# A bidirectional two-branch encoder layer: block products by Strassen's scheme in stages through DRAM

## Chip, cores and metric

One core of one Trainium2 chip. The metric is the device time of one execution of the kernel in microseconds, as the median over runs; lower is better. Engines are named as in the profile: PE is TensorE's matmul, PEld its weight load, DVE is VectorE, ACT is ScalarE, POOL is GpSimd, SP is SyncE, which issues DMAs.

## What is computed

A layer on `x` of 1024 rows (time) by 1024 columns, all in float32:

```
p = x @ w_in                         # 10272 columns in 13 parts
GLA   : 4 heads,  keys 128, values 256; decays log_sigmoid(low-rank @ up + bias) / 16
HGRN2 : 8 heads,  keys 128, values 128; f = lb + (1 - lb) * sigmoid(.), key = 1 - f, decay f
both  : forward and backward chunked linear attention, summed;
        per-head RMSNorm * silu(gate); product with a 1024 x 1024 branch matrix
y   = (sigmoid(m_gla) * y_gla + sigmoid(m_hgrn) * y_hgrn) @ w_out
out = LayerNorm(2 ** 0.25 * x + y)
```

The decays are multiplied up within segments of 64 time steps: with b the running product, `scores = (q * b) (k / b)^T`, masked; a state per chunk carries the rest.

## The kernel before

Class `Layer` does the whole layer in one pass in SBUF. Rows and columns are handled in blocks of 128 (`P`); `T` and `D` are 1024, `KC` and `NT` are 8. `load_x` (L164) keeps x transposed, k on the partitions, as eight pairs of tiles `xh`, `xl`: a float32r part and the rest, made by `split` (L88), a cast on ScalarE (L91) and a subtraction (L92, on GpSimd or VectorE). Each weight block is split in the same way, and a float32 product is formed as three float32r products, hi x hi, hi x lo, lo x hi.

`product_t` (L205) makes a narrow product, 128 output columns by 1024 times: 8 k x 3 terms x 2 halves = 48 matmuls of 512 columns (L216). `narrow` (L221) is called for q and k of the GLA heads, q and the two forget gates of the HGRN heads, and the 16 blocks of merge gates. `wide` (L225) makes 256 output columns with time on the partitions, for values and gates: 2 x 4 x 24 matmuls of 256 columns (L243), sixteen times.

`heads` (L679) goes through four GLA heads, then eight HGRN heads; each head computes its own projections right where it needs them. `scaled` (L339) forms, per direction, the running product of the decays in segments of 64 (a scan, L348, with `FLOOR` to restart each segment), its reciprocal on VectorE in four pieces of 256 columns (L363), the rescaling to the chunk's middle (L364, L365), and the multiplications with q (L366, GpSimd) and k (L368, L370). `attend` (L453) makes masked scores (`scores`, L373), the backward states, then the forward states and the outputs chunk by chunk (`states`, L599; products at L566), the norm and the gate, and transposes the result, which goes to DRAM as `oa` or `oh`. In the GLA heads the values, keys, scores and states are split in halves too (`split_values`, `transposed_halves`, `pieces`) and each of their products is three float32r products; in the HGRN heads they are plain float32.

`branches` (L735) computes merge gates and the two branch products (L216 again), `final` (L777) the output product (L814), residual and LayerNorm. After the heads, `judge` (L838) checks the smallest decay product and the largest mean square; if one is out of bounds, the layer is done again by a slower exact path under `tc.If` (L885).

The order on each engine is set by a scheduler of the framework (L942), from the program's order, from priorities (`high_priority` at L90, L260 and others) and from a simulated timeline. Input loads go over SP's queue; `oa` and `oh` are stored from ScalarE's queue (L531).

Of the kernel before, what the change touches and what calls it, by code (L numbers as in the profile page):

```python
# [9 lines left out]
F32 = mybir.dt.float32  # L10
F32R = mybir.dt.float32r
I32 = mybir.dt.int32
AF = mybir.ActivationFunctionType
ALU = mybir.AluOpType
AX = mybir.AxisListType

P = 128
T = 1024
D = 1024
KC = D // P  # L20
# [26 lines left out]
class Layer:  # L47
    def __init__(self, tc, io, exact):
        self.tc, self.nc, self.io, self.exact = tc, tc.nc, io, exact
# [26 lines left out]
    def t(self, tag, shape=(P, T), dt=F32, name=None):  # L76
        bufs = self.BUFS.get(tag, 1)
        if self.exact and tag in ("PF", "PB"):
            bufs = 1
        return self.sb.tile(list(shape), dt, tag=tag, name=name or tag, bufs=bufs)  # L80
# [4 lines left out]
    def att_ps(self):  # L85
        return self.ps.tile([P, 512], F32, tag="att", name="att", bufs=4)
# [7 lines left out]
    def consts(self):  # L94
        nc = self.nc
        self.ident = self.t("ident", (P, P))
        make_identity(nc, self.ident)
        self.zero = self.t("Z")
        nc.vector.memset(self.zero, FLOOR)
        self.prm = self.t("prm", (P, 43))  # L100
        self.mhalf = self.t("mhalf", (P, NT))
        nc.vector.memset(self.mhalf, -0.5)
        self.minp = self.t("minp", (P, 24))
        self.msall = self.t("msall", (P, 96))
        if self.exact:
            self.level_masks()
        else:
            self.masks()
# [55 lines left out]
    def load_x(self):  # L164
        nc = self.nc
        self.xh, self.xl = [], []
        low = self.io["wn"][0]
        raw = self.raw((P, KC, P))
        hi, lo = self.pair()
        self.ready = [(hi, None)]  # L170
        parts = [slice(0, 2), slice(2, KC)]

        def weights(s):
            nc.sync.dma_start(out=raw[:, s, :], in_=low[:, s, :])
            with self.tc.high_priority():
                nc.scalar.copy(hi[:, s, :], raw[:, s, :])
                nc.gpsimd.tensor_tensor(
                    out=hi[:, s, 96:], in0=raw[:, s, 96:], in1=hi[:, s, 96:].bitcast(F32), op=ALU.subtract
                )

        weights(parts[0])
        for k in range(KC):
            if k % 2 == 0 and k < 4:
                pair = self.t(("gate", "v")[k // 2], (P, 2, T))
            xr = pair[:, k % 2, :] if k < 4 else self.t(("A", "KT", "N0", "N1")[k - 4])
            h = self.t(f"xh{k}", dt=F32R)
            l = self.t(f"xl{k}", dt=F32R)
            for s in (slice(0, 512), slice(512, T)) if k == 0 else (slice(0, T),):
                nc.sync.dma_start(out=xr[:, s], in_=self.io["xT"][k][:, s])
                self.split(h[:, s], l[:, s], xr[:, s], nc.vector)  # L190
            self.xh.append(h)
            self.xl.append(l)
            if k == 1:
                weights(parts[1])
                nc.sync.dma_start(out=self.prm, in_=self.io["prm"])
                self.ready.append(self.weights(self.io["wn"][NARROW.index(A_Q)]))
# [67 lines left out]
    def values(self, column):  # L264
        v = self.t("v", (P, NT, 256))
        for g, ps in self.wide(column):
            with self.tc.high_priority():
                self.nc.scalar.copy(v[:, 4 * g : 4 * g + 4, :], ps)
        return v

    def gates(self, column):
        nc = self.nc
        gate = self.t("gate", (P, NT, 256))
        for g, ps in self.wide(column):
            out = gate[:, 4 * g : 4 * g + 4, :]
            with self.tc.high_priority():
                nc.scalar.activation(out, ps, AF.Sigmoid)
                nc.vector.tensor_tensor(out=out, in0=ps, in1=out, op=ALU.mult)
        return gate
# [59 lines left out]
    def scaled(self, q, k, f, omlb, d, index):  # L339
        nc = self.nc  # L340
        pr = self.t("PB" if d else "PF")
        first, last = (63, 0) if d else (0, 63)
        seg = lambda a: a.rearrange("p (s j) -> p s j", j=64)
        z = self.zero
        nc.vector.tensor_scalar_max(seg(z)[:, :, first], seg(f)[:, :, first], FLOOR)
        nc.vector.memset(seg(f)[:, :, first], 0.0)  # L346
        step = -1 if d else 1
        nc.vector.tensor_tensor_scan(  # L348
            out=pr[:, ::step], data0=f[:, ::step], data1=z[:, ::step], initial=0.0, op0=ALU.mult, op1=ALU.max
        )  # L350
        nc.vector.memset(seg(z)[:, :, first], FLOOR)
        ends = self.t(f"ends{d}", (P, NT, 2))
        nc.vector.tensor_copy(out=ends.rearrange("p c h -> p (c h)"), in_=seg(pr)[:, :, last])
        nc.vector.tensor_reduce(
            out=self.minp[:, index : index + 1], in_=ends.rearrange("p c h -> p (c h)"), axis=AX.X, op=ALU.min
        )
        mid = self.t(f"mid{d}", (P, NT))
        nc.vector.reciprocal(mid, ends[:, :, d])
        half = lambda a: a.rearrange("p (c h j) -> p c h j", h=2, j=64)[:, :, d, :]
        bc = lambda a: a.unsqueeze(2).to_broadcast([P, NT, 64])  # L360
        for n in range(4):
            r = slice(256 * n, 256 * n + 256)
            nc.vector.reciprocal(f[:, r], pr[:, r])  # L363
        nc.vector.tensor_tensor(out=half(f), in0=half(f), in1=bc(ends[:, :, d]), op=ALU.mult)  # L364
        nc.vector.tensor_tensor(out=half(pr), in0=half(pr), in1=bc(mid), op=ALU.mult)  # L365
        nc.gpsimd.tensor_tensor(out=pr, in0=pr, in1=q, op=ALU.mult)  # L366
        if omlb is None:
            nc.vector.tensor_tensor(out=f, in0=f, in1=k, op=ALU.mult)  # L368
        else:
            nc.vector.scalar_tensor_tensor(out=f, in0=f, scalar=omlb, in1=k, op0=ALU.mult, op1=ALU.mult)  # L370
        return pr, f, ends
# [70 lines left out]
    def prepare(self, head, q, kf_of):  # L442
        a = self.t("A") if self.exact else None
        parts = []
        for d in range(2):
            f, k, omlb = kf_of(d)
            if self.exact:
                parts.append(self.exact_dir(a, q, k, f, d, d == 0))
            else:
                parts.append(self.scaled(q, k, f, omlb, d, 2 * head + d))  # L450
        return a, parts
# [112 lines left out]
    def product(self, out, terms):  # L564
        for i, (l, r) in enumerate(terms):
            self.nc.tensor.matmul(out, l, r, start=(i == 0), stop=(i == len(terms) - 1))  # L566
# [80 lines left out]
    def gla_front(self, h):  # L647
        nc = self.nc
        ps = self.narrow(A_Q + P * h)
        q = self.t("Q")  # L650
        with self.tc.high_priority():
            nc.scalar.mul(q, ps, QSCALE)
        fs = self.decays.pop(h) if h in self.decays else self.gla_decays(h)
        ps = self.narrow(A_K + P * h)
        k = self.t("K")
        with self.tc.high_priority():
            nc.scalar.copy(k, ps)
        v = self.values(A_V + 256 * h) if self.exact else self.split_values(A_V + 256 * h)
        prepared = self.prepare(h, q, lambda d: (fs[d], k, None))
        gains = [self.prm[:, 40:41], self.prm[:, 41:42]]  # L660
        rows = [self.oa[2 * h], self.oa[2 * h + 1]]
        return lambda gate: self.attend(h, prepared, v, 0, 256, gate, gains, rows)
# [64 lines left out]
    def merge_gate(self, column, i, sig):  # L727
        ps = self.narrow(column + P * i)
        with self.tc.high_priority():
            self.nc.scalar.activation(sig, ps, AF.Sigmoid)  # L730
# [141 lines left out]
        self.final()  # L872


@with_exitstack
def kernel(ctx: ExitStack, tc: tile.TileContext, xT, x, wn, ww, up_f, up_b, prm, wbg, wbh, w_out, ln_g, ln_b, out):
    io = dict(
        xT=xT, x=x, wn=wn, ww=ww, up_f=up_f, up_b=up_b, prm=prm, wbg=wbg, wbh=wbh, w_out=w_out, ln_g=ln_g, ln_b=ln_b, out=out
    )
    with ExitStack() as inner:  # L880
        fast = Layer(tc, io, False)
        fast.open(inner)
        fast.run()
        bad = fast.unsafe()
    with tc.If(bad > 0):  # L885
        with ExitStack() as inner:
            exact = Layer(tc, io, True)
            exact.open(inner)
            exact.run()
# [56 lines left out]
```

## Time and profile before

| | |
|---|---|
| median of 3 runs | 1405.22 us (1404.96 to 1405.34) |
| the profiled execution's own time | span 1404.6 us from the first to the last instruction |
| busy: PE / PEld | 1369.2 / 1217.4 us |
| busy: DVE / ACT / POOL | 722.5 / 508.6 / 405.9 us |
| instructions | 20453 |
| HBM read / written | 73.16 / 12.58 MB |

How to read it: an engine's busy time is the union of its instructions' spans. Matmuls are pipelined, so that the mean duration of one is longer than the distance from one to the next. A float32 matmul appears as two records, a float32r one as one. A group names the tile written, then the tiles read, with partitions x elements and type; behind the bar it has busy time and mean duration, then the idle time before it. The window table has a column per engine, the granted clock of TensorE as a share of full speed, the DMA engines' busy share and the bytes moved.

### The profile page before, as it was taken

The page shows a single profiled execution, that of the slowest core. Times are in us where ns is not written, and L with a number is a line of the kernel's source. Part 1 is how long each engine was busy: PE and PEld are TensorE (multiplying, and loading weights), DVE is VectorE, ACT ScalarE, POOL GpSimd, SP SyncE. Part 2 cuts the span into 40 slices and gives each one's busy share as a digit, 9 for nine tenths or more (in the row PEclk, how much of TensorE's full clock was granted, in tenths as well). Part 3 has the DMA queues.
Part 4 walks back from the last instruction along what each step waited for, and adds up shares of the span by engine and source line. Part 5 has one row for each costly group of instructions (what it writes and reads, how often), then busy time and mean ns, then how long its engine had stood idle before and what let it go on. Part 6 is the DMA issues. An engine that isn't in the chain of part 4 may idle for free.

```text
span 1404.6 us, 20453 instructions
## 1 busy us (share of the span) xinstructions
PE 1369.2 (97%) x8721; PEld 1217.4 (87%) x8721; DVE 722.5 (51%) x993; ACT 508.6 (36%) x822; POOL 405.9 (29%) x262
## 2 busy tenths in 40 slices
PE   8999999999999999999999999999999999999996
PEld 6989979989999889888988898988888888888886
DVE  5886478296255575557545654565311132123744
ACT  6445365454453434334333443243421031113100
POOL 3334425326233231323132313222222222221111
PEclk9999999999999999999999999999999999999998
DMA  6010110210112110211021102011231151113421
GB/s 224 25 46 31 61 46 16 76 46 31 61 47 75 46 46 16 76 46 45 16 76 31 60 16 76 31 46 60 91 105 45 46 177 48 45 46 105 136 105 63
DMA packets 24405, 87.16 MB, mean 62 GB/s; under 512 B 2928, under 2 KB 3056, under 8 KB 24304
## 3 DMA queue, kind: packets, MB, share of 16 engines
q1 hardware_dynamic: 22000, 77.36, 16.6%
q10 hardware_dynamic: 2304, 8.39, 1.6%
q8 instruction: 70, 1.15, 0.3%
q14 instruction: 31, 0.25, 0.1%
HBM read 73.16 MB, written 12.58 MB: 61 GB/s over the span
## 4 chain that ended last, share of the span: by engine, by line
PE 66%; DVE 16%; POOL 5%; issue 5%; ACT 5%; DMA 3%; SPq 0%; POOLq 0%; DVEq 0%; ACTq 0%
PE proj L216 35%; PE proj L243 13%; PE att L566 7%; PE proj L814 5%; DVE FF L363 4%; DMA wraw<-in_dram 3%; DVE FB L363 2%; POOL PB L366 2%; PE att L382 2%; POOL wlo L92 2%; DVE PF L348 2%; ACT whi L91 1%; POOL PF L366 1%; PE att L540 1%; DVE PB L348 1%
## 5 line engine op out<-in xcount | busy, mean ns | idle before, releaser
L92 POOL TENSOR_TENSOR wlo<-wraw,whi 128x1024 fp32r<-128x1024 f32 x78 | 187.4, 2402 | 447.7 <-ACT whi L91 447.7
L243 PE MATMUL proj<-whi,xh 128*128 128x256 f32 x1024 | 291.2, 284 | 1.5 <-DVE v L261 1.5
L243 PE MATMUL proj<-wlo,xh 128*128 128x256 f32 x1024 | 291.1, 284 | 0.2 <-POOL wlo L92 0.2
L243 PE MATMUL proj<-whi,xl 128*128 128x256 f32 x1024 | 291.2, 284 | 0.0
L216 PE MATMUL proj<-xh,whi 128*128 128x512 f32 x768 | 243.7, 395 | 0.7 <-DVE FB L346 0.5
L216 PE MATMUL proj<-xl,whi 128*128 128x512 f32 x768 | 241.5, 394 | 0.0
L216 PE MATMUL proj<-xh,wlo 128*128 128x512 f32 x768 | 239.4, 391 | 0.0
L91 ACT CAST whi<-wraw 128x1024 fp32r<-128x1024 f32 x78 | 81.9, 1050 | 357.9 <-PE proj L216 176.9
L243 PEld LDWEIGHTS proj<-whi,xh 128*128 128x128 f32 x1024 | 196.1, 191 | 2.6 <-DVE v L261 2.0
L243 PEld LDWEIGHTS proj<-wlo,xh 128*128 128x128 f32 x1024 | 196.1, 191 | 1.2 <-POOL wlo L92 0.5
L243 PEld LDWEIGHTS proj<-whi,xl 128*128 128x128 f32 x1024 | 196.1, 191 | 0.0
L216 PEld LDWEIGHTS proj<-xh,wlo 128*128 128x128 f32 x768 | 144.2, 188 | 30.3 <-POOL wlo L92 0.3
L216 PEld LDWEIGHTS proj<-xh,whi 128*128 128x128 f32 x768 | 143.3, 189 | 30.3 <-ACT whi L91 0.9
L216 PEld LDWEIGHTS proj<-xl,whi 128*128 128x128 f32 x768 | 143.5, 189 | 29.4 <-issue 0.7
L92 POOL TENSOR_TENSOR wlo<-N,whi 128x1024 fp32r<-128x1024 f32 x18 | 43.7, 2429 | 149.7 <-ACT whi L91 149.7
L363 DVE RECIPROCAL FF<-PF 128x256 f32<-128x256 f32 x48 | 79.7, 1707 | 0.1
L363 DVE RECIPROCAL FB<-PB 128x256 f32<-128x256 f32 x48 | 79.7, 1708 | 0.1
L366 POOL TENSOR_TENSOR PB<-PB,Q 128x1024 f32<-128x1024 f32 x12 | 41.5, 3457 | 83.6 <-DVE PB L365 81.0
L91 ACT CAST whi<-N 128x1024 fp32r<-128x1024 f32 x19 | 19.9, 1050 | 106.2 <-PE proj L216 56.4
L566 PE MATMUL att<-v,KT 128*128 128x128 f32 (+1 forms) x392 | 56.1, 282 | 0.8 <-DVE KT L557 0.7
L631 ACT ACTIVATE V<-att,ends 128x128 f32<-128x128 f32 (+1 forms) x144 | 54.5, 392 | 6.0 <-PE att L566 5.9
L566 PEld LDWEIGHTS att<-v,KT 128*128 128x128 f32 x392 | 51.8, 194 | 3.3 <-DVE KT L557 1.7
(364 smaller groups left out, 2173.5 us busy)
## 6 DMA issues: line engine op xcount, KB each, us to landing
wraw<-in_dram SPq DMA_DIRECT2D x82, 512.0 KB, 3.5
N<-in_dram SPq DMA_DIRECT2D x24, 512.0 KB, 3.5
oa<-KT ACTq DMA_DIRECT2D x8, 512.0 KB, 3.3
oh<-KT ACTq DMA_DIRECT2D x8, 512.0 KB, 3.4
whi<-in_dram SPq DMA_DIRECT2D x8, 512.0 KB, 3.5
out_dram<-wlo SPq DMA_DIRECT2D x7, 512.0 KB, 2.6
v<-oh SPq DMA_DIRECT2D x4, 512.0 KB, 5.4
v<-in_dram SPq DMA_DIRECT2D x2, 512.0 KB, 7.6
```

The source lines that it names most:

```text
L91: nc.scalar.copy(hi, raw)
L92: (lo_engine or nc.gpsimd).tensor_tensor(out=lo, in0=raw, in1=hi.bitcast(F32), op=ALU.subtract)
L216: nc.tensor.matmul(out, w[:, k, :], x[k][:, 512 * n : 512 * n + 512], start=(i == 0), stop=(i == len(terms) - 1))
L243: nc.tensor.matmul(ps[:, 256 * j : 256 * j + 256], x[k][:, P * c : P * c + P], w[k], start=(k == 0 and i == 0), stop=(k == KC - 1 and i == 2),
L348: nc.vector.tensor_tensor_scan(out=pr[:, ::step], data0=f[:, ::step], data1=z[:, ::step], initial=0.0, op0=ALU.mult, op1=ALU.max)
L363: nc.vector.reciprocal(f[:, r], pr[:, r])
L366: nc.gpsimd.tensor_tensor(out=pr, in0=pr, in1=q, op=ALU.mult)
L382: mm = lambda out, l, r: nc.tensor.matmul(out, l, r, start=True, stop=True)
L540: nc.tensor.transpose(out=pt[:, P * j : P * j + P], in_=k[:, s], identity=self.ident)
L566: self.nc.tensor.matmul(out, l, r, start=(i == 0), stop=(i == len(terms) - 1))
L631: nc.scalar.mul(new, u, mul[:, c, near : near + 1])
L814: nc.tensor.matmul(pss[n], y[k][:, s], w[k][:, cuts[n]], start=(i == 0), stop=(i == len(terms) - 1))
```

## The change

A class `Fast(Layer)` takes over the first pass; the exact path stays. The work is done in three stages with their own SBUF pools, with q, keys, logarithms of decays, values, gates, raw merge gates and the GLA half of the sum passing through DRAM:

1. `dense`: all projections but the merge gates. Two column blocks are taken together, so that each product is a 2 x 2 block product (weights' halves of k by two blocks; halves of k by halves of time), done with seven block products and sums of operands and results (`sums`, `operands`, `seven`). Sixteen narrow jobs, then eight wide ones, each preparing the next job's weights ahead. Sigmoids, logarithms and gates are applied here, and the results stored. x is kept as seven split operands of four chunks.
2. `heads`: the attention heads in the order `SEQUENCE`, HGRN and GLA mixed, with one or two merge gates (plain products, 48 matmuls each) after most of them, from `MERGES`. Decays are summed as logarithms (the scan now has ones, zero at each segment's start, as multiplier), and the exponentials of the sum and of its negative are taken on ScalarE in place of reciprocals. GLA heads are computed in plain float32 like the HGRN heads. New states are written to new tiles.
3. `last_stage`: eight branch jobs and four jobs of the output product, again with seven block products.

All loads and stores go over SP's queue. The core of the diff:

```diff
+class Fast(Layer):
+    ORDER = ("P1", "P6", "P2", "P7", "P5", "P4", "P3")
+    KEPT = ("P1", "P2", "P3")
...
+    def sums(self, a11, a12, a21, a22, width):
...
+        s1, s2 = s(), s()
+        v.tensor_tensor(out=s1, in0=a21, in1=a22, op=ALU.add)
+        v.tensor_tensor(out=s2, in0=s1, in1=a11, op=ALU.subtract)
...
+            self.split(hi, lo, raw)
+            made[name] = (hi, lo)
+
+        put("P1", a11)
+        put("P6", s2)
+        put("P2", a12)
+        s3 = s()
+        v.tensor_tensor(out=s3, in0=a11, in1=a21, op=ALU.subtract)
+        put("P7", s3)
+        put("P5", s1)
+        put("P4", a22)
+        s4 = s()
+        v.tensor_tensor(out=s4, in0=a12, in1=s2, op=ALU.subtract)
+        put("P3", s4)
...
+    def operands(self, load, unit):
...
+        engines = [nc.vector, nc.gpsimd]
...
+        for k in range(4):
+            b11, b12, b21, b22 = load(k, 0), load(k, 1), load(k + 4, 0), load(k + 4, 1)
+            t1, t2, t3, t4 = (self.t("s", (P, self.slot))[:, 0:512] for _ in range(4))
+            put("P1", k, b11, k)
+            with self.tc.high_priority():
+                nc.vector.tensor_tensor(out=t1, in0=b12, in1=b11, op=ALU.subtract)
+                nc.vector.tensor_tensor(out=t2, in0=b22, in1=t1, op=ALU.subtract)
+            put("P6", k, t2, 0)
+            put("P2", k, b21, 1)
+            with self.tc.high_priority():
+                nc.vector.tensor_tensor(out=t3, in0=b22, in1=b12, op=ALU.subtract)
+                nc.vector.tensor_tensor(out=t4, in0=t2, in1=b21, op=ALU.subtract)
+            put("P7", k, t3, 1)
+            put("P5", k, t1, 0)
+            put("P4", k, t4, 1)
+            put("P3", k, b22, 1)
...
+    def narrow_product(self, w, x):
...
+            terms = [(k, i, j) for k in range(4) for i, j in ((0, 0), (0, 1), (1, 0))]
...
+    def seven(self, product, count, out):
...
+        product(x, "P1")
+        with first():
+            for n in pieces:
+                nc.scalar.copy(e[n], x[n])
+        product(y, "P6")
+        with first():
+            add(u, y, e)
+        product(x, "P2", True)
+        with first():
+            for n in pieces:
+                out(0, 0, n, x[n], True)
+        product(y, "P7", True)
+        with first():
+            add(v, y, e)
+        z = banks()
+        product(z, "P5")
+        with first():
+            add(e, z, v)
+            for n in pieces:
+                out(1, 1, n, e[n], False)
+        p = banks()
+        product(p, "P4")
+        with first():
+            add(v, v, p, ALU.subtract)
+            for n in pieces:
+                out(1, 0, n, v[n], False)
+        product(z, "P3", True)
+        with first():
+            add(u, u, z)
+            for n in pieces:
+                out(0, 1, n, u[n], False)
...
+    def narrow_job(self, kind, at, w):
...
+        self.seven(self.narrow_product(w, self.xs), 1, out)
+        for i, col, s in late:
...
+            nc.gpsimd.tensor_scalar(out=k, in0=s, scalar1=self.nomlb[:, n : n + 1], scalar2=o, op0=ALU.mult, op1=ALU.add)
+            self.store(self.ks[GLA_HEADS + n][:, col], k)
+            nc.scalar.activation(s, s, AF.Ln, scale=o, bias=b)
+            self.store(self.logs[2 * (GLA_HEADS + at) + i][:, col], s)
...
+    def dense(self):
...
+        self.counts = {"raw": 5, "s": 3, "w": 8, "h": 14}
...
+    def scaled(self, q, k, f, unit, d, index):
...
+        nc.vector.tensor_tensor_scan(
+            out=pr[:, ::step],
+            data0=self.runs,
+            data1=f[:, ::step],
+            initial=0.0,
+            op0=ALU.mult,
+            op1=ALU.add,
+        )
...
+        nc.scalar.activation(f, pr, AF.Exp, scale=-unit)
+        nc.scalar.activation(pr, pr, AF.Exp, scale=unit)
+        nc.gpsimd.tensor_tensor(out=pr, in0=pr, in1=q, op=ALU.mult)
+        nc.vector.tensor_tensor(out=f, in0=f, in1=k, op=ALU.mult)
...
+    SEQUENCE = ("H0", "H1", "A0", "H2", "H3", "A1", "A2", "H4", "H5", "A3", "H6", "H7")
+    MERGES = (2, 1, 2, 1, 2, 2, 1, 1, 2, 2, 0, 0)
...
+    def branch_job(self, x, w, pair, last):
...
+            g = tiles[i, j]
+            o = slice(512 * j, 512 * j + 512)
+            engine = nc.vector if psum else nc.gpsimd
+            engine.tensor_tensor(out=g, in0=c, in1=g, op=ALU.mult)
+            if last:
+                nc.vector.tensor_tensor(out=y[:, pair[i], o], in0=y[:, pair[i], o], in1=g, op=ALU.add)
+            else:
+                self.store(self.ya[pair[i]][:, o], g)
...
+    def last_stage(self):
...
+        self.counts = {"raw": 2, "s": 4, "w": 5, "h": 8, "sig": 4}
...
+        for n, (b, pair) in enumerate(jobs):
+            if n % 4 == 0:
+                x = self.second(self.rows_of((self.oa, self.oh)[b]))
...
+            ahead = weights(n + 1) if n + 1 < len(jobs) else None
+            self.branch_job(x, ready, pair, b)
...
-    with ExitStack() as inner:
-        fast = Layer(tc, io, False)
-        fast.open(inner)
-        fast.run()
-        bad = fast.unsafe()
+    fast = Fast(tc, io)
+    fast.run()
+    bad = fast.unsafe()
```

`second` builds the operands of the branch outputs or of the output weights in the same tiles, one per name and chunk; the banks `x`, `y`, `z`, `p` of `seven` come from eight PSUM banks, and `e`, `u`, `v` and the loaded pieces share the tag "h".

## Rows read from the trace of the kernel before

**Rows 1.** The page's head and its first part: busy time of each engine.
```profile
span 1404.6 us, 20453 instructions
...
PE 1369.2 (97%) x8721; PEld 1217.4 (87%) x8721; DVE 722.5 (51%) x993; ACT 508.6 (36%) x822; POOL 405.9 (29%) x262
```

**Rows 2.** Stretches: us, then PE, PEld, DVE, ACT, POOL busy, clock, DMA, GB/s.
```profile
0.00:15.00 15.00, 8.62 (x19) 5.14 (x19) 8.70 (x15) 9.11 (x12) 5.42 (x15) 1.00 0.85 311
...
15.00:440.00 425.00, 416.81 (x3098) 388.64 (x3097) 264.39 (x364) 213.55 (x343) 157.51 (x118) 1.00 0.16 53
...
440.00:1004.00 564.00, 554.67 (x3847) 499.64 (x3846) 330.31 (x499) 218.36 (x400) 166.28 (x87) 1.00 0.14 47
...
1004.00:1382.00 378.00, 378.00 (x1671) 313.04 (x1670) 107.75 (x98) 67.55 (x67) 73.25 (x38) 1.00 0.26 86
...
1382.00:1404.60 22.60, 11.15 (x93) 10.94 (x91) 11.39 (x20) 0.00 (x0) 3.44 (x4) 0.83 0.13 50
```

**Rows 3.** The chain that ended last, in time: start us, us, what.
```profile
41.03 21.61 PE proj L243 x180
...
1003.72 301.74 PE proj L216 x1331
```

**Rows 4.** Groups of PE by shape: busy us, mean ns, idle before.
```profile
L243 PE MATMUL proj<-whi,xl 128*128 128x256 f32 x1024 | 291.2, 284 | 0.0
...
L216 PE MATMUL proj<-xh,whi 128*128 128x512 f32 x768 | 243.7, 395 | 0.7 <-DVE FB L346 0.5 <-ACT whi L91 0.2
```

**Rows 5.** Timeline of PE in an HGRN head: start us, us, instruction, records.
```profile
493.05 0.39 PE L566 MATMUL att<-Sf,PF 128*128 128x128 f32 x2
...
493.27 0.39 PE L566 MATMUL att<-v,A 128*128 128x128 f32 x2
```

**Rows 6.** Groups of ACT, POOL and DVE by shape, same columns.
```profile
L91 ACT CAST whi<-wraw 128x1024 fp32r<-128x1024 f32 x78 | 81.9, 1050 | 357.9 <-PE proj L216 176.9
...
L92 POOL TENSOR_TENSOR wlo<-wraw,whi 128x1024 fp32r<-128x1024 f32 x78 | 187.4, 2402 | 447.7 <-ACT whi L91 447.7
...
L363 DVE RECIPROCAL FF<-PF 128x256 f32<-128x256 f32 x48 | 79.7, 1707 | 0.1
...
L366 POOL TENSOR_TENSOR PB<-PB,Q 128x1024 f32<-128x1024 f32 x12 | 41.5, 3457 | 83.6 <-DVE PB L365 81.0
...
L365 DVE TENSOR_TENSOR PB<-PB,mid 128x512 f32<-128x512 f32 x12 | 8.2, 685 | 0.0
...
L366 POOL TENSOR_TENSOR PF<-PF,Q 128x1024 f32<-128x1024 f32 x12 | 38.0, 3165 | 22.4 <-DVE PF L365 14.3 <-DVE FB L346 8.1
...
L513 POOL TENSOR_TENSOR rs<-msall,mhalf 128x4 f32<-128x4 f32 x16 | 16.1, 1008 | 1.3
...
L513 POOL TENSOR_TENSOR rs<-msall,mhalf 128x2 f32<-128x2 f32 x16 | 11.6, 724 | 1.3
```

**Rows 7.** Timeline of DVE and POOL in the branch products.
```profile
1165.32 2.93 DVE L761 TENSOR_TENSOR N<-Z,N 128x1024 f32<-128x1024 f32 x1
...
1298.02 1.22 DVE L761 TENSOR_TENSOR Q<-Z,Q 128x1024 f32<-128x1024 f32 x1
...
1164.78 2.39 POOL L92 TENSOR_TENSOR wlo<-N,whi 128x1024 fp32r<-128x1024 f32 x1 [8.49 <-ACT whi L91]
```

**Rows 8.** Waits of PE: us in total, times, longest us.
```profile
PE att L382 <- POOL PB L366: 9.3, 8, 1.8
...
PE att L554 <- DVE sq L393: 3.4, 2, 1.7
```

**Rows 9.** DMA issues with KB and us to landing; one SP issue.
```profile
wraw<-in_dram SPq DMA_DIRECT2D x82, 512.0 KB, 3.5
...
3.12 0.43 SPq L195 DMA_DIRECT2D prm<-in_dram  x1
```

**Rows 10.** Timeline of PE at the start: pairs of products.
```profile
9.63 1.22 PE L216 MATMUL att<-xl,whi 128*128 128x512 f32 x2
...
22.28 0.62 PE L216 MATMUL proj<-xh,whi 128*128 128x512 f32 x2
```

547 lines of the change are left out of this document (added), and 3 rows, old and new, of the table BUFS.

## The prediction

> **What bounds the kernel now.** I read the page's first part first. TensorE is busy 1369.2 of 1404.6 us, VectorE 722.5, ScalarE 508.6, GpSimd 405.9 [rows 1]: one engine is the bound, and what the others save is worth nothing until it waits for them. The table by stretches says where TensorE still waits [rows 2]: 6.4 us at the start, 8.2 in the GLA heads, 9.3 in the HGRN heads, nothing in the branch and output products, 11.4 at the end. They make 35.3 us; the rest of the span can only shrink if TensorE gets less to do. The profiled span stands 0.6 us under the 1405.2 us median, so I sum against the span and add 0.6. About 0.2%, 2.8 us, is what a measurement here can tell from no change.
>
> Next, what one matmul costs. A single duration overlaps its neighbours, so I take uninterrupted runs from the chain [rows 3]: 301.74 us for 1331 products of 512 columns is 0.2267 us each, 21.61 us for 180 of 256 columns is 0.120. Groups by shape give the counts [rows 4]: three forms of 1024 wide products, three of 768 narrow ones. With the code: narrow 48 x 48 = 2304 and branches 16 x 48 = 768 of 512 columns, wide 3072 of 256, the last stage 336 of 512 and 96 of 256, the low-rank product 32 and its use 16. So 696.4 + 368.6 + 76.2 + 11.5 + 10.9 = 1164 us of dense work, and 1369 - 1164 = 205 us of attention.
>
> **TensorE's work after the change.** Seven products replace eight in everything but the merge gates.
> - Narrow projections: 16 jobs of 7 x 12 = 84 matmuls, 1344 in place of 1536: 192 x 0.2267 = -43.5 us.
> - Wide ones: 8 jobs of 7 x 48 = 336, 2688 in place of 3072: 384 x 0.120 = -46.1.
> - Branches: 8 x 84 = 672 in place of 768: -21.8.
> - Last stage: 4 x 84 = 336 of 512, where 76.2 + 11.5 stood: -11.5.
> - Low rank: 40 for 32: +1.8.
> - GLA attention loses its halves: 14 + 22 products a head, each three products of split halves with 256 columns (3 x 0.120 = 0.36) that become one in float32. A float32 product of 128 columns takes 0.22 us [rows 5], so 256 take about 0.45 (ends: 0.36, as cheap as now, and 0.45, the columns doubled). I take the upper, the multiple of the form shown: 144 x 0.09 = +13.
>
> Sum -108, TensorE 1261 us. By stage: projections 16 x 19.0 + 8 x 40.3 + 13 = 640; heads 205 + 13 + 768 x 0.2267 (merge gates) = 392; last stage 12 x 19.0 = 229.
>
> **What the other engines get, and what TensorE waits for.** Splitting stays a ScalarE cast (1.05 us for 1024 columns) and a subtraction, 2.40 us on GpSimd [rows 6]; for 512 columns I halve both. VectorE's 512-column operation takes 0.69. A narrow job of 19.0 us has seven splits and on VectorE four operand sums and five sums of products: ScalarE under 12 us with a decay's sigmoids and logarithms, GpSimd 8.4 (plus four two-scalar operations in a decay job, priced nowhere: nothing to 1.2 us each, taken as 1.2, the two-input form), VectorE 6.2. All lie beside TensorE. A wide job of 40.3 us has 7 x 2.40 = 17 on GpSimd, about 17 on VectorE, 13 on ScalarE. The cover holds on average; what isn't covered:
> - **Start.** The first product needs four chunks of x, and each chunk is turned into seven split operands before the next. Up to the last chunk's first operand GpSimd does seven weight splits and some 14 of x, 21 x 1.2 = 25 us behind the first load of some 3; now 15 us hold 6.4 idle [rows 2]. I take 27 us idle (ends 15, with the orders interleaved well, and 35, with all 25 subtractions ahead).
> - **Couplings in a job.** P2 adds onto the bank of P1 once ScalarE has copied it, P7 and P3 onto banks VectorE has just read; between lies one product, 2.7 us, against 0.53 and 0.69. That hides them unless something is queued ahead. The trace shows what can be: a VectorE sum of two SBUF operands takes 1.22 us alone and 2.93 when GpSimd's 2.39 us subtraction runs [rows 7], a delay of 1.65, for 512 columns 0.83. Four sums a job over 28 narrow, branch and last jobs would be 93 us of VectorE if each met one; behind 2.7 us of cover I take 12 (ends 0 and 93).
> - The Trainium skill, "GPSIMD Engine Reference" (Specifications), says that GpSimd's SBUF interfaces are shared with VectorE and that VectorE instructions with two SBUF inputs contend there. The trace agrees, 1.22 against 2.93 us [rows 7]. With the rule at its worst for every sum the total would be 81 us higher, without it 12 lower.
> - **Heads.** With products of 800 us among them TensorE waited 9.3 + 3.4 = 12.7 us for the heads' own chains [rows 8]. Now only merge gates lie between, 174 us, under half of the stage. VectorE loses the reciprocals (1.71 us, eight a head [rows 6]): 330.3 us over eight heads [rows 2] less 13.7 each leaves at most 27.6 a head, some 340 for twelve, under 392. I take the waits doubled, 25 us (ends 13 and the second rival). The logarithms' exponentials, four a head of some 1 us like its casts [rows 6], go to ScalarE, which was busy 218 of 564 us there.
> - **Changes of operand in the last stage.** The operands of the HGRN branch and of the output weights reuse the tiles of the running ones, with eight load tiles, so most can be built only as the last job with the old ones ends. 18 subtractions on GpSimd are 21.6 us beside a job's 12 of 19.0; I take 10 us a change, 20 (ends 0 and 43). The first change lies under the last two heads.
> - **End.** The same chain of additions, statistics and one store: 11 us [rows 2].
> - **DMA.** Staging projections, decays, gates and the half sum through DRAM adds 118 MB (59 MB of q, k, decays, values, gates and half sums, written and read) to what is moved now at 47 to 53 GB/s; the start moved 311 GB/s [rows 2], the average here would be about 150. Some 600 issues on SP at about 0.4 us [rows 9] fill under a fifth of it; stores that wait for results stand ahead of loads there, but a landing is 3.5 us [rows 9] and loads are a job or a head ahead. Nothing (ends 0 and 3.5 a head, 42).
>
> Sum: 1261 + 27 + 12 + 25 + 20 + 11 = 1356, plus 0.6: **1357 us**, 3.4% below before.
>
> **Rivals.**
> - **The cover holds everywhere.** Idle time as before, 35, plus some 10 for the longer start: 1261 + 45 = 1306. For it: no other engine's count exceeds TensorE's in any stage. Against: two operand changes and the start have a count that cannot hide.
> - **VectorE and GpSimd take turns in the heads** (slower). GpSimd's multiplications (41.5 + 38.0 us), powers (16.1 + 11.6) and 32 merge-gate splits (38) are 145 us [rows 6]. If VectorE can do none of its two-operand work beside them, the stage is 340 + 145 = 485 in place of 392 + 25: 1357 + 68 = 1425. It decides once more than 77 of those 145 us collide (340 + 77 = 417). For: scans, key products and state updates all read two SBUF operands. Against: VectorE also reads PSUM, and the engines have free time to shift into.
> - **The clock falls in the heads** (slower too). The first products take 1.22 us a pair, later 0.62 [rows 10], though the record grants 1.00 there; in the last stretch the granted clock is 0.83 as TensorE stops [rows 2]: of the levels 1.2 and 2.4 GHz, the lower after idling. Were a quarter of the heads' 392 us at 1.2 GHz, +98: 1455. Against: the clock stayed 1.00 between 15 and 1382 us in spite of waits [rows 2].
> - The Trainium skill, "TensorE: Matmul & The Clock Gate" (The HAM clock gate), says that idling throttles the array to half and activity releases it, and that gaps between bursts pay this again each time. The falling clock at the end agrees; no row shows it between heads.
>
> That the exact path runs as well is not a rival: the same decays are judged against the same bound, and the span before holds one pass.
>
> **How the numbers follow.** Forecast 0.60, cover 0.22, turns 0.11, clock 0.07. The forecast's unknown ends reach from about 1320 to 1400. Below 1300 lies nearly half of the second case, above 1414 most of the last two: range 1300 to 1414. Faster by over 0.2%: 0.82 (the first two cases); within 0.2%: 0.03; slower: 0.15, nearly all of the last two.
>
> **What would show it.** 2688 wide, 1344 + 672 + 336 narrow seven-product matmuls and 768 for merge gates, at 0.120 and 0.227; TensorE busy about 1261; a first 30 us nearly empty of products; a heads stage of 415 to 420 us with waits for GpSimd and VectorE; two gaps of some 10 us in the last stage. Wrong: TensorE busy above 1300, a granted clock under 0.97 in the heads, or gaps in the projections above 20 us in all.

## The result and the profile after

The changed kernel takes 1546.18 us (1543.54 to 1549.0, 4 runs) against 1405.28 us: ratio 1.1003, 95% interval 1.0983 to 1.1024. The forecast was 1357 us. It is 10% slower, and 189 us above the forecast.

The page of the kernel after: span, busy times, and two lines of the table in 40 slices (tenths of TensorE's busy share, tenths of the granted clock), which answer to [rows 1].

```profile
span 1547.3 us, 21052 instructions
...
PE 1349.3 (87%) x7817; PEld 1140.9 (74%) x7817; DVE 887.3 (57%) x1147; ACT 702.4 (45%) x1240; POOL 803.2 (52%) x561
...
PE   4899999999999999994999989998676797696495
...
PEclk9899999999999999996999999999778799698698
```

TensorE is still the fullest engine, but at 87% where it was at 97%, and its busy time is 1349 us where the counts of matmuls promised 1261. GpSimd's time has doubled, from 406 to 803 us. The slices show where: nines from the third slice to the middle, a hole at the seam between projections and heads, and a ragged last third, with a lower clock under each hole.

The same by stages, to be laid beside [rows 2] (us, then PE, PEld, DVE, ACT, POOL busy with instructions, granted clock, DMA share, GB/s): start, projections, seam, heads while merge gates last, heads without, last stage, end.

```profile
0.00:50.00 50.00, 23.83 (x64) 13.54 (x64) 36.00 (x37) 21.59 (x38) 39.41 (x36) 0.99 0.45 158
50.00:697.00 647.00, 636.21 (x4024) 577.44 (x4024) 284.88 (x326) 295.91 (x402) 326.72 (x203) 0.99 0.36 121
697.00:720.00 23.00, 2.83 (x8) 1.45 (x6) 22.26 (x27) 11.61 (x17) 8.79 (x6) 0.59 1.00 388
720.00:1080.00 360.00, 339.98 (x2130) 279.58 (x2130) 205.47 (x328) 181.57 (x406) 142.35 (x109) 0.97 0.42 148
1080.00:1195.00 115.00, 82.42 (x584) 69.10 (x584) 81.64 (x152) 72.95 (x175) 40.41 (x36) 0.81 0.33 110
1195.00:1533.00 338.00, 263.92 (x1010) 199.75 (x1009) 249.02 (x269) 118.82 (x205) 242.33 (x169) 0.85 0.40 129
1533.00:1547.30 14.30, 0.15 (x1) 0.00 (x0) 8.06 (x14) 0.00 (x0) 3.23 (x4) 0.65 0.29 78
```

Subtract busy from length in each row: TensorE idles 26 us at the start, 11 in the projections, 20 at the seam, 20 and 33 in the heads, 74 in the last stage, 14 at the end: 198 in all, where 95 were forecast. The other 88 us are busy time above the counted work (20 up to 697 us, 33 in the heads, 35 in the last stage). 198 - 95 + 88 = 191 us; the profiled span stands 191 above the forecast sum of 1356.

Groups of TensorE in the kernel after, by shape, answer to [rows 4].

```profile
L995 PE MATMUL bank<-xP,w 128*128 128x512 f32 x1344 | 324.3, 401 | 35.0 <-ACT xP L91 21.1 <-DVE h L1029 4.9 <-DVE xP L92 4.5
L1008 PE MATMUL bank<-w,xP 128*128 128x256 f32 x2688 | 322.9, 283 | 0.0
L995 PE MATMUL bank<-P,w 128*128 128x512 f32 x1008 | 263.7, 420 | 71.4 <-ACT P L91 25.2 <-ACT w L91 16.4 <-DVE P L92 14.1
```

The counts are those forecast: 1344, 2688, and 672 + 336 = 1008. The wide group takes 322.9 us for the 322.6 counted. The last one, in the last stage, takes 263.7 for 228.5 counted, and the engine idles 71.4 us in front of its instructions, mostly for the casts (L91) and subtractions (L92) of operands. There are three changes of operands in this stage, and none is hidden. The rows of the three stretches, same columns as above:

```profile
1195.00:1240.00 45.00, 30.04 (x87) 19.99 (x87) 41.68 (x38) 21.98 (x38) 37.83 (x24) 0.72 0.34 117
1300.00:1350.00 50.00, 31.18 (x77) 17.66 (x78) 41.00 (x35) 23.18 (x41) 44.45 (x28) 0.69 0.49 168
1412.00:1457.00 45.00, 10.87 (x27) 5.92 (x26) 41.89 (x36) 19.79 (x34) 35.50 (x23) 0.57 0.32 100
```

TensorE idles 15, 19 and 34 us in them, 68 of the stage's 74. Of the first 15, 4 are waits for the check of the bounds (`judge`).

The third change, in the timeline (start us, us, instruction, idle time before it): first TensorE, then VectorE and GpSimd in the same stretch.

```profile
1421.21 1.22 PE L995 MATMUL bank<-P,w 128*128 128x512 f32 x2 [3.63 <-POOL P L92]
1425.13 0.79 PE L995 MATMUL bank<-P,w 128*128 128x512 f32 x1 [2.70 <-ACT P L91]
1430.13 1.22 PE L995 MATMUL bank<-P,w 128*128 128x512 f32 x2 [4.21 <-DVE P L92]
```

```profile
1418.27 1.76 DVE L982 TENSOR_TENSOR s<-h 128x512 f32<-128x512 f32 x1
1419.95 1.75 DVE L92 TENSOR_TENSOR P<-s,P 128x512 fp32r<-128x512 f32 x1
1421.63 0.67 DVE L1029 TENSOR_TENSOR h<-h,bank 128x512 f32<-128x512 f32 x1
...
1431.69 0.68 DVE L92 TENSOR_TENSOR P<-s,P 128x512 fp32r<-128x512 f32 x1
...
1417.76 5.08 POOL L92 TENSOR_TENSOR P<-h,P 128x512 fp32r<-128x512 f32 x3
...
1433.01 1.69 POOL L92 TENSOR_TENSOR P<-h,P 128x512 fp32r<-128x512 f32 x1 [1.80 <-ACT P L91]
```

VectorE's operation with two SBUF inputs takes 1.75 us while GpSimd works and 0.68 in the gap after 1431.2; the one with a PSUM input at 1421.63 takes 0.67 in the middle of it all. GpSimd's pieces take 1.7 us, against 1.2 forecast from [rows 6]. TensorE gets one or two products every four to six microseconds, and then waits once for 13.9 us, until the first weights of the output product are cast.

### The profile page after: what moved, and what is told of

Same layout as the page of the kernel before. It is cut to its first block, busy times and chain, and to the rows that moved or that the text cites. A ratio compares the mean times of both kernels' runs of the same rounds, so it can differ in the third digit from the quotient of the medians.

```text
span 1547.3 us, 21052 instructions
## 1 busy us (share of the span) xinstructions
PE 1349.3 (87%) x7817; PEld 1140.9 (74%) x7817; DVE 887.3 (57%) x1147; ACT 702.4 (45%) x1240; POOL 803.2 (52%) x561
## 5 line engine op out<-in xcount | busy, mean ns | idle before, releaser
L995 PE MATMUL bank<-xP,w 128*128 128x512 f32 x1344 | 324.3, 401 | 35.0 <-ACT xP L91 21.1
L92 POOL TENSOR_TENSOR w<-s,w 128x512 fp32r<-128x512 f32 (+1 forms) x144 | 235.0, 1635 | 192.8 <-ACT w L91 189.1
L995 PEld LDWEIGHTS bank<-xP,w 128*128 128x128 f32 x1344 | 256.5, 192 | 100.8 <-ACT xP L91 25.2
L995 PE MATMUL bank<-P,w 128*128 128x512 f32 x1008 | 263.7, 420 | 71.4 <-ACT P L91 25.2
L1008 PEld LDWEIGHTS bank<-w,xP 128*128 128x128 f32 x2688 | 322.8, 192 | 0.2
L1008 PE MATMUL bank<-w,xP 128*128 128x256 f32 x2688 | 322.9, 283 | 0.0
L995 PEld LDWEIGHTS bank<-P,w 128*128 128x128 f32 x1008 | 199.6, 201 | 135.3 <-ACT P L91 34.7
L92 POOL TENSOR_TENSOR w<-raw,w 128x512 fp32r<-128x512 f32 (+1 forms) x96 | 156.5, 1631 | 137.8 <-ACT w L91 112.7
L91 ACT CAST w<-s 128x512 fp32r<-128x512 f32 (+1 forms) x144 | 101.7, 713 | 155.9 <-PE bank L1008 68.4
L1029 DVE TENSOR_TENSOR h<-bank,h 128x512 f32<-128x512 f32 x132 | 90.7, 688 | 131.6 <-PE bank L1008 77.2
L1286 PE MATMUL proj<-xP,hw 128*128 128x512 f32 x576 | 153.3, 408 | 1.9 <-POOL hw L92 1.6
L1286 PEld LDWEIGHTS proj<-xP,hw 128*128 128x128 f32 x576 | 106.6, 192 | 25.2 <-POOL hw L92 2.7
L91 ACT CAST w<-raw 128x512 fp32r<-128x512 f32 (+1 forms) x96 | 69.5, 724 | 115.5 <-issue 66.6
L1029 DVE TENSOR_TENSOR h<-h,bank 128x512 f32<-128x512 f32 x88 | 60.0, 682 | 66.9 <-PE bank L995 35.1
L92 POOL TENSOR_TENSOR hw<-hraw,hw 128x512 fp32r<-128x512 f32 x32 | 46.4, 1455 | 71.0 <-ACT hw L91 71.0
L382 PE MATMUL sc<-PF,FF 128*64 128x64 f32 (+1 forms) x384 | 46.9, 267 | 25.1 <-POOL PF L1340 20.1
```

The costliest lines, as they stand in the source:

```text
L91: nc.scalar.copy(hi, raw)
L92: (lo_engine or nc.gpsimd).tensor_tensor(out=lo, in0=raw, in1=hi.bitcast(F32), op=ALU.subtract)
L382: mm = lambda out, l, r: nc.tensor.matmul(out, l, r, start=True, stop=True)
L995: self.nc.tensor.matmul(out[0], a[i][:, k, :], b[k][:, j, :], start=(n == 0 and not more), stop=(n == len(terms) - 1), skip_group_check=True,)
L1008: self.nc.tensor.matmul(out[c // 2][:, 256 * (c % 2) : 256 * (c % 2) + 256], b[k][:, j, P * c : P * c + P], a[i][:, k, :], start=(n == 0 a ...
L1029: nc.vector.tensor_tensor(out=to[n], in0=one[n], in1=two[n], op=op)
```

## Experiments

Theory A: three things cost time. In the last stage, each of three matrices has to be turned into 28 split operands with 16 sums in the tiles in use, on two engines that take turns. In the heads, TensorE has nothing dense left to do between the heads' chains. Long gaps also lower the clock. The seven products pay only where the operands are made once. Rivals stand with each run.

**Plain last stage** (eight block products and no sums in the last stage, two sets of operand tiles):

```diff
+    def eight(self, product, count, out):
+        for i, first, second in ((0, "P1", "P2"), (1, "P5", "P4")):
+            for j, top, low in ((0, "P1", "P2"), (1, "P6", "P3")):
+                x = [self.bank() for _ in range(count)]
+                product(x, (first, top))
+                product(x, (second, low), True)
...
-        return self.operands(load, lambda name, k: self.t(f"{name}{k}", (P, 2, 512), F32R))
+        return self.operands(load, lambda name, k: self.t(f"{name}{k}", (P, 2, 512), F32R, bufs=2))
...
-        self.counts = {"raw": 2, "s": 4, "w": 5, "h": 8, "sig": 4}
+        self.plain = True
+        self.counts = {"raw": 2, "w": 5, "h": 4, "sig": 4}
```

> Plain products (eight block products, no sums of operands) in the last stage alone, with two sets of operand tiles: 16 split operands a matrix in place of 28, and TensorE 12 x 96 matmuls in place of 12 x 84. Theory A (TensorE starves in the last stage because 28 split operands and 16 sums a matrix have to be rebuilt in the very tiles in use): TensorE's 261 us plus some 15 for the first operands and 14 at the end make the stage about 290 us in place of 360, the whole about 1475 us. Rival B (the stage waits for what stays: stores and loads on one queue, gates, weights): 33 us more of TensorE come on top, about 1575 us.

Measured 1473.36 us, ratio to before 1.0482 (1.046 to 1.0504): 73 us less than the changed kernel, with 144 matmuls more. Its last stage and end, same columns as above:

```profile
1191.00:1462.00 271.00, 265.59 (x1152) 217.44 (x1152) 103.13 (x138) 74.58 (x126) 106.76 (x85) 0.98 0.52 169
1462.00:1472.70 10.70, 0.00 (x0) 0.00 (x0) 4.33 (x7) 0.00 (x0) 1.70 (x2) 0.74 0.19 55
```

1152 products in 271 us where 1008 took 338. VectorE and GpSimd drop to 103 and 107 us from 249 and 242. Theory A's number holds; rival B is out.

**One set of tiles** for the same plain stage (`bufs=1`, eight load tiles), to part the tiles from the amount of work:

> The kernel with the plain last stage, but with one set of operand tiles, as the changed kernel has. Theory A (what costs is the number of splits and sums that must pass between two matrices, 28 and 16 against 16 and none): a change costs some 8 us, three of them part hidden: 1480 to 1495 us. Rival B (what costs is that the tiles in use must come free first): most of the 73 us that the plain last stage saved come back: above 1515 us.

Measured 1485.44 us, ratio 1.0575 (1.0557 to 1.0592). That is theory A's range; rival B is out. Of the 73 us, 12 come with the second set of tiles and 61 with fewer splits and no sums. The 61 are net: the plain stage also has 144 more products, 33 us of TensorE at 0.227 each.

**GpSimd's low parts made elsewhere.** Two runs test that the two engines take turns. In the first, the 18 low parts of an operand set that GpSimd made are copies on ScalarE (the subtraction is left out):

```diff
+            if self.late and n % 2:
+                with self.tc.high_priority():
+                    nc.scalar.copy(u[:, 0, :], raw)
+                    nc.scalar.copy(u[:, 1, :], raw)
```

> In the last stage the 18 low parts of each operand set that GpSimd made are ScalarE copies of the raw piece (the subtraction is left out). Theory A, VectorE and GpSimd take turns: VectorE's two-operand work there returns from 1.2 to 1.75 us to 0.69, each of the three operand changes shrinks by 10 to 15 us: 1505 to 1515 us. Rival B, what counts is that pieces and temporaries wait for their tiles and loads: within 8 us of 1546.

Measured 1521.78 us, ratio 1.0828 (1.081 to 1.0846): 24 us less, short of theory A's 31 to 41, three times rival B's bound. VectorE's busy time in the stage falls from 249 to 206 us. In the second, those subtractions and the ones of the weights go to VectorE, the fuller engine:

```diff
-        engines = [nc.vector, nc.gpsimd]
+        engines = [nc.vector, nc.vector if self.late else nc.gpsimd]
...
-            self.split(hi, lo, raw)
+            self.split(hi, lo, raw, self.nc.vector if self.late else None)
```

> In the last stage of the changed kernel every subtraction of a split is VectorE's, none GpSimd's. Theory A (the two take turns, so GpSimd's 1.29 us pieces cost VectorE more than its own 0.69 would): the sum of both in the stage falls from some 400 to 315 us and the stage with it, 1500 to 1515 us. Rival B (they work side by side, and VectorE at 277 us busy is the fuller one): 138 more operations of 0.69 us make the stage VectorE's, above 1555 us.

Measured 1522.48 us, ratio 1.084 (1.0822 to 1.0858). Its last stage:

```profile
1195.00:1505.00 310.00, 258.03 (x1009) 199.99 (x1009) 253.39 (x399) 116.12 (x201) 42.92 (x38) 0.87 0.42 138
```

VectorE runs 399 instructions here where it ran 269, and is busy 253 us where it was 249. The subtraction of a temporary, by its line (minimum / median / maximum ns):

```profile
L92 DVE TENSOR_TENSOR P<-s,P x48: 670/679/694, 1196.4 to 1424.9; 128x512 fp32r<-128x512 f32 x48
```

0.68 us each time. The 130 more instructions are 88 us of that; so the work that took VectorE 249 us beside GpSimd takes some 165 without. A third of that busy time was waiting, then, and more work made the engine hardly fuller. Had the two worked side by side (rival B), the stage should have become longer. The gain is again 24 us and not 31 or more. What remains is put down to the amount, with VectorE busy 253 us of 310 and the run on one set of tiles beside it; no run takes it apart further. By the Trainium skill, "GPSIMD Engine Reference" (Specifications), the two share SBUF interfaces and contend where VectorE has two SBUF inputs; 0.68 against 1.75 us agrees.

**Merge gates later.** `MERGES = (1, 1, 1, 1, 2, 1, 1, 1, 2, 1, 2, 2)`:

> The sixteen merge gates spread to the end of the heads (1,1,1,1,2,1,1,1,2,1,2,2 in place of 2,1,2,1,2,2,1,1,2,2,0,0). Theory A: between 1077 and 1187 us TensorE has no merge gate left, is busy 74% and falls to the lower clock; four gates there save about 20 us, 1525 us. Rival B: the gates are only moved, gaps open earlier in the stage by as much as close at its end: 1540 to 1552 us.

Measured 1535.04 us, ratio 1.0923 (1.089 to 1.0956): 11 us less, half of what theory A expected, and below rival B. But the run did not do what it was meant to. By the line of the gates' products (minimum / median / maximum ns, first to last start)

```profile
L1286 PE MATMUL proj<-xP,hw x576: 387/389/797, 717.4 to 1065.9; 128*128 128x512 f32 x192
```

the last gate starts at 1065.9 us, and so even before the 1076.7 us of the changed kernel: the scheduler drew the gates forward, and the end of the heads stayed bare. By its rows 8 of the 11 us lie in the heads after 1080 us (107 us in place of 115); why is left open, and the run says nothing on either theory.

**No seven products at all**, stages and DRAM as they are:

> No seven-product scheme anywhere; stages, DRAM, heads and logarithms as they are. Theory A (in the projections the seven products pay, in the last stage they cost): the projections end 35 us later less 8 us of a shorter start, the last stage is 70 us shorter: about 1503 us. Rival B (the scheme pays or costs nothing in the projections either): as the kernel with a plain last stage, within 8 us.

Measured 1528.19 us, ratio 1.0871 (1.0852 to 1.0891): 55 us above the kernel with a plain last stage alone, where I expected 28. So in the projections the seven products pay. By the rows, 44 of the 55 us are the later end of the projections; 10 more are a longer heads stage (504 us against 494), whose code is the same in both, and they stay unexplained. The rows of this kernel show what the staging alone does (start, projections, heads, last stage):

```profile
0.00:50.00 50.00, 39.79 (x163) 32.40 (x164) 13.48 (x18) 30.13 (x46) 35.70 (x38) 1.00 0.70 244
50.00:741.00 691.00, 691.00 (x4495) 635.55 (x4493) 49.61 (x72) 225.64 (x304) 181.54 (x119) 1.00 0.33 111
741.00:1245.00 504.00, 434.97 (x2722) 357.23 (x2721) 306.84 (x501) 264.01 (x593) 186.91 (x145) 0.92 0.39 139
1245.00:1515.00 270.00, 265.27 (x1152) 217.35 (x1152) 103.50 (x137) 75.31 (x127) 107.37 (x86) 0.98 0.52 171
```

The start idles 10 us in place of 26, the projections not at all and end 44 us later. The heads, 392 us of work by count, take 504. Not only the seven products cost time, then: the division into stages, with the new order of work, does as well.

**Values between the heads** (plain products again, a group of heads ahead, on top of the plain last stage; four tiles for split weights, two for keys):

```diff
-        v = self.t("v", (P, NT, 256))
-        self.nc.sync.dma_start(out=v.rearrange("p c e -> p (c e)"), in_=self.staged[column])
+        self.ready_v = self.values(next(columns))
         for name, count in zip(self.SEQUENCE, self.MERGES):
             (self.gla_front if name[0] == "A" else self.hgrn_front)(int(name[1]))
+            if name in firsts:
+                column = next(columns, None)
+                if column is not None:
+                    self.ready_v = self.values(column)
```

> The kernel with the plain last stage, and the values' projections taken out of the first stage: plain products between the heads, each a group of heads ahead, the first one at the stage's start. Theory A (the heads starve for lack of dense work between them): the first stage is 161 us shorter, the heads stage takes the 184 us of products into its gaps and is about 110 us longer: about 1420 us. Rival B (the heads stage is as long as its own chains, whatever lies between): it grows by the full 184 us: about 1496 us.

Measured 1450.78 us, ratio 1.0322 (1.0305 to 1.0339): 23 us less than without, between the two, though the plain values are 23 us more work for TensorE (184 against 161). With the gates spread as well:

> The same with the merge gates spread to the end of the heads. Theory A: 10 us less than the kernel with the values between the heads, as in the run that only spread the gates: about 1410 us. Rival B: with the values there the gaps at the end are the last heads' own chains: no change, within 4 us.

Measured 1435.11 us, ratio 1.0213 (1.0196 to 1.023): 16 us less, and this time the gates do run on to 1137 us; rival B is out. The rows show both why it works and why it isn't more (end of the projections, seam, heads, seam):

```profile
50.00:536.00 486.00, 471.40 (x2681) 413.76 (x2680) 236.69 (x272) 257.78 (x357) 260.42 (x175) 0.99 0.36 125
536.00:580.00 44.00, 24.24 (x172) 22.51 (x173) 31.73 (x30) 14.82 (x22) 23.64 (x12) 0.73 0.66 232
580.00:1140.00 560.00, 553.72 (x4071) 497.44 (x4070) 259.41 (x458) 280.36 (x628) 200.95 (x160) 1.00 0.33 111
1140.00:1157.00 17.00, 4.18 (x20) 2.64 (x18) 5.68 (x17) 5.63 (x10) 8.61 (x9) 0.61 0.62 211
```

With dense work between them the heads keep TensorE busy 554 of 560 us at a clock of 1.00. What is left are the seams, 20 and 13 us idle, and the start's 26 us as in the changed kernel.

**The logarithms alone**, in the kernel before (scan of logarithms, exponentials on ScalarE, no reciprocals; nothing else):

```diff
-        for n in range(4):
-            r = slice(256 * n, 256 * n + 256)
-            nc.vector.reciprocal(f[:, r], pr[:, r])
...
+        nc.scalar.activation(f, pr, AF.Exp, scale=-unit)
+        nc.scalar.activation(pr, pr, AF.Exp, scale=unit)
```

> The kernel before with the decays by sums of logarithms alone (no reciprocals on VectorE, exponentials and logarithms on ScalarE). Theory A: TensorE stays the bound and VectorE's 160 us were beside it: 1400 to 1409 us. Rival B: the 12.7 us that TensorE waited for the heads' chains go: 1391 to 1397 us. Rival C: ScalarE's table changes and exponentials lengthen those chains: above 1412 us.

Measured 1384.95 us, ratio 0.9854 (0.9838 to 0.9871): beyond rival B's range on its side. This version beats both kernels. Its busy times, and what TensorE still waits for:

```profile
PE 1362.7 (99%) x8721; PEld 1215.8 (88%) x8721; DVE 536.7 (39%) x779; ACT 624.7 (45%) x940; POOL 385.1 (28%) x262
```

```profile
PE att L217 <- ACT xh L91: 6.5, 2, 5.4
PE att L379 <- POOL PB L363: 2.2, 3, 0.7
```

VectorE is relieved of 186 us. The heads' waits of [rows 8] are down to 2.2 us, and TensorE's idle time from 35 to 20. That is 15 us of the 21 by which the span shrinks. The other 6 are in its busy time, 1362.7 for 1369.2 with the same 8721 records. Half of these lie in the score products (L382 before, L379 here): 37.1 us for 40.5.

**GLA heads in plain float32**, on top of that:

> The kernel before with the logarithms, and the GLA heads' products in plain float32 in place of three products of halves. Theory A (TensorE is the bound; a float32 product of 256 columns costs 0.43 to 0.45 us against 0.36): 144 products, 10 to 13 us more than with the logarithms alone, 1395 to 1398 us. Rival B (the splits that go free other engines and with them TensorE): 1381 to 1389 us.

Measured 1393.28 us, ratio 0.9917 (0.9901 to 0.9934): 8.3 us more than with the logarithms alone. Theory A's sign, a little under its size, and above rival B's range; the busy time of TensorE grows by as much, 1371.0 for 1362.7.

## Why the prediction was wrong

The steps of the prediction that failed: it priced every matmul at the full clock and as part of a stream (88 us of busy time above the count); it gave changes of operand 20 us, where the last stage idles 74; it gave the heads 25 us of waiting, where they idle 73 with the seam; and it put the logarithms at nothing, which are a gain of 20. None of its slower rivals had the last stage in it, and the slowest, 1455, lies below the 1546 measured.

The runs give a ledger in which every step is a difference of two medians, so that it must add up: the logarithms -20, plain float32 in the GLA heads +8, staging through DRAM with its new order of work +135 (1528.2 against 1393.3), the seven products in the projections -55, in the last stage +73 of which 12 are the single tiles. The 135 were never taken apart: stages, traffic through DRAM, order of the heads and place of the gates changed together. Most of them lie in the heads, which take 504 us there for 392 counted.

- **TensorE's work** was right in count. The 13 us for GLA's float32 products measured 8.3. Busy time missed by 88 us all the same. Of these, 58 are the clock: the trace grants 0.50 in 211 us of the span (so its mean is 0.932), TensorE is busy in 117 of them, and at the full clock it would have needed half. The rest is in the main the start, where pairs take 1.22 us while the profile shows 1.00, and products that run alone, which count with their whole duration and not with the 0.227 us of a stream. In the last stage the clock stands at 0.50 while operands are changed and TensorE works 4 of 20 us, and at 1.00 forty microseconds later (rows of 20 us of the kernel after):

```profile
1420.00:1440.00 20.00, 4.26 (x7) 1.81 (x8) 19.91 (x16) 7.01 (x12) 17.80 (x11) 0.50 0.44 133
...
1460.00:1480.00 20.00, 20.00 (x89) 16.52 (x88) 17.21 (x22) 5.46 (x9) 14.27 (x12) 1.00 0.29 83
```

  0.50 is 1.2 GHz, of 2.4. I gave this mechanism 0.07 as a rival and only in the heads, arguing from a trace in which TensorE was hardly ever short of work. Even there the clock did not stay at 1.00 throughout, as I had read from the long rows of [rows 2]; a shorter row of the kernel before, same columns:

```profile
260.00:350.00 90.00, 87.85 (x667) 81.34 (x667) 61.74 (x87) 45.90 (x78) 33.18 (x27) 0.98 0.13 42
```

  The lower clock is not a rival to the gaps but their companion: in the run with the values and the late gates, the row with next to no gaps (580 to 1140 us above) has 1.00. The Trainium skill, "TensorE: Matmul & The Clock Gate" (The HAM clock gate), says that bursts with gaps between pay for the ramp again each time; the trace agrees, with 117 us of work at 0.50.
- **Changes of operand**, 20 us for two: this term was the most mis-sized, and its upper end of 43 too. The first change, which I had put under the last two heads, idles 15 us, the second 19, the third 34. I counted GpSimd's 18 subtractions beside the rest. But 16 sums, 10 subtractions on VectorE and 18 on GpSimd take turns where they meet, the job's own splits among them. The stage idles 74 us and is busy 35 us above its count. I had used the very row that shows the collision [rows 7], for the couplings inside a job, and given it its full weight only as a rival in the heads; it decided in the last stage. There the two runs that took GpSimd out of it gain 24 us, and the plain stage with its fewer splits and no sums 61, probably with these 24 among them.
- **Heads**, 25 us: measured 73 idle with the seam, and 33 of busy time above the count. Doubling the waits of before assumed that 174 us of merge gates would cover as 800 us of products did. They covered while they lasted (340 of 360 us busy) and were used up at 1077 us. The seam, 20 us in which the first heads scan and exponentiate with nothing for TensorE to do, had no term at all (start us, us, instruction, idle time before it):

```profile
699.44 2.29 DVE L1320 TENSOR_TENSOR_SCAN PF<-runs,FF 128x1024 f32<-128x1024 f32 x1
...
711.35 1.04 ACT L1338 ACTIVATE FF<-PF 128x1024 f32<-128x1024 f32 x1
...
714.82 2.35 POOL L1340 TENSOR_TENSOR PF<-PF,Q 128x1024 f32<-128x1024 f32 x1
...
717.23 0.69 PE L382 MATMUL sc<-PF,FF 128*64 128x128 f32 x2 [20.09 <-POOL PF L1340]
```

- **The logarithms** I costed at nothing, as time moved beside TensorE. They are worth 20 us in the kernel before. The argument that other engines' savings are worth nothing was too strong: the heads' chains ended last 12.7 us in [rows 8], and a shorter chain frees them.
- **Start and end**: 27 and 11 forecast, 26 and 14 measured. The start's number is partly luck: GpSimd was busy without a break from 10 us to 43 as forecast, but its pieces took up to 1.7 us, not 1.2, and TensorE got products in between. **Couplings**, 12 forecast for all jobs: TensorE waits 12.8 us for VectorE's additions (L1029) and 3.6 for ScalarE's copy (L1036) in the whole kernel. That the projections idle 11 us in all is another count.
- **DRAM traffic**: HBM moved 204 MB, the forecast's 118 on top of 86, and 132 GB/s; at the seam DMA was busy throughout (388 GB/s), elsewhere no more than half. TensorE's one long wait there ended on GpSimd's product above and not on a load; whether the loads delayed what led up to it was not tried apart.

Of the signs of being wrong that I had named, two came, TensorE busy above 1300 us and a clock under 0.97 in the heads (0.81 after 1080 us); gaps of 20 us in the projections did not. One figure was also added wrongly: 27.6 us a head are 331 for twelve, not some 340, which changes nothing.

## What to carry to other kernels

A scheme that saves multiplications is paid for in operand preparation: count the sums and splits per reuse of an operand, and price VectorE's and GpSimd's together where both read two SBUF inputs. Here it paid where x was prepared once for 24 jobs, and cost 73 us where a matrix served four. Work taken out from between latency chains has to leave cover behind, gap by gap, since a long gap here cost its length and then some work at half the clock. And test the small part of a bundle alone: here the logarithms, which I had put at nothing, were a gain of 20 us by themselves.

## What the runs showed of the hardware beyond expectation

- Not only VectorE waits: GpSimd's pieces slow down as well when VectorE works on two SBUF inputs, from 1.29 us alone to 1.7 in most collisions, for 128x512. One that began just before VectorE's operation kept its 1.29 (start us, us, instruction; the second piece of GpSimd's is one alone):

```profile
1399.86 1.76 DVE L1509 TENSOR_TENSOR Y<-Y,sig 128x512 f32<-128x512 f32 x1 [1.19 <-POOL sig L1507]
...
1399.79 1.29 POOL L92 TENSOR_TENSOR w<-s,w 128x512 fp32r<-128x512 f32 x1
1402.62 1.29 POOL L92 TENSOR_TENSOR w<-raw,w 128x512 fp32r<-128x512 f32 x1 [1.54 <-ACT w L91]
```

- A float32 product of 256 columns takes 0.43 to 0.44 us, start to start, in the changed kernel; start us, us, records:

```profile
1128.58 0.59 PE L566 MATMUL po<-v,A 128*128 128x256 f32 x2
1129.02 0.59 PE L566 MATMUL po<-Sb,PB 128*128 128x256 f32 x2
1129.45 1.46 PE L566 MATMUL st<-v,KT 128*128 128x256 f32 x6
```

  Twice the 0.22 of [rows 5], as estimated. Over the 0.36 of three products of halves that is 11 us for 144, of which 8.3 arrived in the time.
